# A hybrid decoder trunk on one core: channel sums as one matmul, pooling sums in banks of their own, the last convolution behind the pooling

## The chip, the cores and the metric

The kernel runs on one core of a Trainium2 chip. The metric is device time in microseconds (us), the median of the runs of one kernel on the chip. The engines are PE (TensorE matmuls), PEld (TensorE weight loads), DVE (VectorE), ACT (ScalarE), POOL (GpSimd) and SP (SyncE, which issues most DMAs). Each engine works through its own queue in order and waits on semaphores for the others.

## The reference

One layer for 288 tokens: 256 of a prompt and 8 × 4 sample tokens, which have a history.

```python
h = rmsnorm(x, norm1_g)
proj = h @ w_in + b_in                                  # 2048 -> 3072
a, gate, z = proj[:1024], proj[1024:2048], proj[2048:]  # columns
u = a * sigmoid(gate)
c = silu(layernorm(depthwise_causal_conv(history + u, conv_w (31 taps), conv_b), ln_g, ln_b))
d = multiscale_pool(history + z)      # windows 2, 4, 8, 16 for four groups of 256 channels: window mean - z
p = (d per group @ pool_w[g]) * pool_scale
x = x + concat[c, p] @ w_out                            # 2048 -> 2048
x = x + relu(rmsnorm(x, norm2_g) @ w_ff1) ** 2 @ w_ff2  # 2048 -> 8192 -> 2048
y = rmsnorm(x, norm_f)
```

`rmsnorm` divides by the root of the mean square over the 2048 channels, `layernorm` over the 1024 of the convolution. The outputs are y, the last 30 u and the last 15 z per sequence.

## The kernel before

Channels lie on the 128 partitions, the 288 tokens along the free dimension, so x is 16 tiles (xT) of 128x288. All matmuls take weights of 128x128 as the stationary operand and 288 tokens as the moving one, and fill a PSUM bank `ac` of 128x288. Numbers are split into two parts of a faster format: ScalarE casts a weight block of 128x1024 to `whi` (line 235), VectorE or GpSimd subtracts it from the original to give `wlo` (line 236), and each product is three matmuls, hi × hi, lo × hi, hi × lo (lines 242 to 244). Activations are split the same way (hh and hl, dh and dl, ph and pl, mh and ml, ah and al, fh and fl). There are four buffers each of whi and wlo, four PSUM banks `ac`, two banks `cv` and two banks `ms`.

The order of work on TensorE, in blocks of 256 output columns (a gemm):

- a first stage of 8 steps c, two input tiles each, for convolution channels 0 and 1 (`first_banks`, line 314). x and weights come in together, step by step. 12 warming matmuls of two passes each run ahead of it;
- gemms for conv 2 to 7 (`CONVS`), each giving a and gate of 128 channels, then for pool groups 3, 2, 1, 0 (`POOLS`), 96 matmuls each;
- the pool matmuls of the four groups, 12 each;
- w_out: eight groups of 48 matmuls on the pooling half (bringing in ph and pl), then eight on the convolution half (mh and ml), each added to xT;
- four rounds of ff1 (eight groups) and ff2 (eight groups), 96 matmuls a group.

The norms' factors are applied behind the matmuls. For that, `rsqrt_rows` needs a sum over channels and a root for each of the 288 tokens. It sums with one-column matmuls (`pt`, line 203; three of 96 tokens, on 96 partitions), takes the root on 96x3 elements with a Newton step (lines 211 to 218, tile `st`), writes the result on a diagonal (`dg`, line 220) and spreads it to all partitions with a matmul (`pr`, line 227). It is used four times: for rb (first norm), for the layernorm in w_out (`norm_end`), for r2 (ff1) and for the final norm (rf).

A convolution's gate (`conv_gates`) multiplies both banks by rb, takes the sigmoid `tg` and writes u into `uz`. The 31 taps (`conv_taps`, line 368) then run on VectorE, two channels' chains in turns, with a low priority; their sums end in the tiles `c`, and GpSimd adds these up to `sum_c`. `pmean` (line 440) averages sum_c over channels in w_out's third group. A pool group (`pool_group`) multiplies its bank by rb, writes z to uz, and then puts the windows' sums into the same bank b (line 407), down to dl (line 415).

The program is written in this order, but a scheduler places instructions on each engine's queue by its own estimate of times and by priorities; buffers of a pool are handed out as they come free.

Of the kernel before, what the change touches and what calls it, by code (L numbers as in the profile page):

```python
# [21 lines left out]
TB = T // 3  # L22
# [19 lines left out]
CONVS, POOLS = (2, 3, 4, 5, 6, 7), (3, 2, 1, 0)  # L42
GROUPS = (3, 2, 1, 0)


def weight_blocks():
# [6 lines left out]
    for i in CONVS:  # L53
        yield from w_in(i * P, DC + i * P)
    for g in POOLS:
        yield from w_in(2 * DC + 2 * g * P, 2 * DC + (2 * g + 1) * P)
# [23 lines left out]
def trunk_kernel(ctx: ExitStack, tc: tile.TileContext, io):  # L80
# [58 lines left out]
    squares = uz[:, 0 : KT * T].rearrange("p (k t) -> p k t", t=T)  # L139
# [19 lines left out]
    def load_first(c, cuts=((0, 2),)):  # L159

        raw = raw_tile()
        to = raw[:].rearrange("p (b k) n -> p b k n", b=2)
        src = io["w"][2 * (c // 4) : 2 * (c // 4) + 2].rearrange("b p k n -> p b k n")
        for k0, k1 in cuts:
            nc.sync.dma_start(xT[:, 2 * c + k0 : 2 * c + k1, :], io["xT"][:, 2 * c + k0 : 2 * c + k1, :])
            at = 2 * (c % 4)
            nc.sync.dma_start(to[:, :, k0:k1, :], src[:, :, at + k0 : at + k1, :])
        return raw
# [13 lines left out]
    few = const.tile([P, 1], F32, name="few")  # L182

# [6 lines left out]
    for j in range(12):  # L190
        nc.tensor.matmul(warm[:, 0:P], ones, ones, start=True, stop=True)
    ident = const.tile([TB, TB], F32, name="ident")
    make_identity(nc, ident)
# [5 lines left out]
    def token_sums(parts, pt):  # L199

        for j in range(3):
            for n, t in enumerate(parts):
                nc.tensor.matmul(pt[:TB, j : j + 1], t[:, j * TB : (j + 1) * TB], ones[:, 0:1], start=n == 0, stop=n == len(parts) - 1)  # L203

    def rsqrt_rows(parts, scale, after=None):

        pt = ms("pt", 3)
        token_sums(parts, pt)
        st = const.tile([TB, 4, 3], F32, name=nm("st"))
        s = [st[:, n, :] for n in range(4)]  # L210
        nc.vector.tensor_scalar(s[0], pt[:TB, 0:3], scale, EPS, op0=ALU.mult, op1=ALU.add)
        nc.scalar.activation(s[1], s[0], AF.Sqrt)
        if after is not None:
            load_table(after, s[1][:, 0:1])
        nc.vector.reciprocal(s[2], s[1])
        nc.vector.tensor_tensor(s[3], s[2], s[2], op=ALU.mult)
        nc.vector.scalar_tensor_tensor(out=s[3], in0=s[3], scalar=-0.5, in1=s[0], op0=ALU.mult, op1=ALU.mult)  # L217
        nc.vector.scalar_tensor_tensor(out=s[2], in0=s[3], scalar=1.5, in1=s[2], op0=ALU.add, op1=ALU.mult)
        dg = tmp("dg")
        nc.vector.tensor_tensor(  # L220
            dg[:TB, :].rearrange("p (j t) -> p j t", t=TB),
            ident[:, None, :].to_broadcast([TB, 3, TB]),
            s[2][:, :, None].to_broadcast([TB, 3, TB]),
            op=ALU.mult,
        )
        pr = ms("pr")
        nc.tensor.matmul(pr[:, :T], ones[:TB, :], dg[:TB, :], start=True, stop=True)  # L227
        return pr
# [17 lines left out]
    def gemm(banks, rhs, m_outer=False):  # L246
# [6 lines left out]
        for k, m in order:  # L253
            product(banks[m], rhs[k], get(k, m), k == 0, k == n - 1)
# [12 lines left out]
    def weight_groups():  # L267

        V, G = nc.vector, nc.gpsimd
        for _ in range(len(CONVS) + len(POOLS)):  # L270
            yield halves([split(raw, G) for _ in range(2) for raw in load()])
# [14 lines left out]
    first_banks = bank2() + [bank("cv", cvp, "cv") for _ in range(2)]  # L286
    for c in range(8):
        pair = []
        for k in range(2 * c, 2 * c + 2):
            hh, hl = act("hh"), act("hl")  # L290
            nc.scalar.activation(hh, xT[:, k, :], AF.Copy, scale=v("norm1_g", k))
            nc.vector.scalar_tensor_tensor(out=hl, in0=xT[:, k, :], scalar=v("norm1_g", k), in1=f32(hh), op0=ALU.mult, op1=ALU.subtract)
            pair.append((hh, hl))
        raw = first_raw[c]
        if c == 0:
            hi = wspl.tile([P, 4, 256], F32R, name=nm("whi"), tag="whi")
            lo = wspl.tile([P, 4, 256], F32R, name=nm("wlo"), tag="wlo")
            views = [t[:].rearrange("p (b k) n -> p b k n", b=2) for t in (raw, hi, lo)]
            for k in range(2):
                r, h, l = [t[:, :, k, :] for t in views]  # L300
                nc.scalar.copy(h, r)
                nc.vector.tensor_tensor(l, r, h.bitcast(F32), op=ALU.subtract)
        else:
            hi, lo = split(raw, nc.vector if c < 5 else nc.gpsimd)
# [73 lines left out]
    for i in CONVS:  # L378
# [5 lines left out]
        if i % 2:  # L384
            conv_taps((i - 1, i))
# [209 lines left out]
```

## Time and profile before

| | |
|---|---|
| median of 3 runs | 1130.59 us (1129.89 to 1130.7) |
| profiled execution | 1128.56 us, span 1126.4 us |
| TensorE busy | 1095.7 us, 97% |
| VectorE busy | 643.2 us, 57% |
| ScalarE busy | 473.1 us, 42% |
| GpSimd busy | 173.8 us, 15% |
| mean granted TensorE clock | 0.986 |

The span is the part that the profiler records, from the first to the last instruction; the profiled execution's own time lies 2.2 us around it. Shares are averages over the span. Matmul durations overlap, so TensorE's pace is read from counts over a stretch of time. In rows of groups, the columns are busy time and mean duration in ns of one, and behind the last bar the idle time ahead of them with what ended it. In rows of time, they are the start, the duration, and in brackets the idle time before and its releaser.

### The profile page before, as it was taken

What the parts mean: (1) busy time and instruction counts of PE and PEld (TensorE: products, weight loads), DVE (VectorE), ACT (ScalarE), POOL (GpSimd) and SP (SyncE); (2) the same over time, 40 slices, a digit from 0 to 9 for tenths busy, and PEclk for the clock granted to TensorE, in tenths of its full rate; (3) what the DMA queues carried; (4) which work ended last, traced back from release to release, by engine and by line L of the source; (5) the groups of instructions that cost most, each with busy time, mean ns of one, the idle gap of its engine ahead of it and who ended that gap; (6) DMA issues with size and microseconds to landing.
All of it is one profiled execution on the core that took longest, in us unless ns stands there. A gap on an engine that the chain in (4) does not pass through costs nothing.

```text
span 1126.4 us, 19701 instructions
## 1 busy us (share of the span) xinstructions
PE 1095.7 (97%) x8182; PEld 1090.9 (97%) x8182; DVE 643.2 (57%) x974; ACT 473.1 (42%) x650; POOL 173.8 (15%) x111
## 2 busy tenths in 40 slices
PE   9899968999999999999999999999999999999995
PEld 8899968999999999999999999999999999999995
DVE  7699999477655444444455444454544444554553
ACT  8443434465454433334444333444433334444441
POOL 3899945820000000000000000000000000000000
PEclk9999988999999999999999999999999999999998
DMA  9655726555555555555555555555555555555532
GB/s 322 205 167 171 212 95 156 159 166 165 167 167 165 161 165 168 168 169 166 162 166 164 166 169 168 166 166 162 165 166 169 168 165 163 167 165 166 168 95 84
DMA packets 56665, 187.04 MB, mean 166 GB/s; under 512 B 5888, under 2 KB 11008, under 8 KB 56576
## 3 DMA queue, kind: packets, MB, share of 16 engines
q1 hardware_dynamic: 56432, 185.74, 52.9%
q8 instruction: 64, 1.05, 0.4%
q14 instruction: 25, 0.20, 0.0%
q10 hardware_dynamic: 144, 0.05, 0.0%
HBM read 181.49 MB, written 4.28 MB: 165 GB/s over the span
## 4 chain that ended last, share of the span: by engine, by line
PE 93%; DVE 4%; DMA 1%; issue 1%; ACT 0%; SPq 0%; DVEq 0%
PE ac L242 31%; PE ac L244 31%; PE ac L243 30%; DVE pc L368 1%; DVE ac L407 1%; PE ac L314 1%; PE cv L314 1%; DMA xT<-in_xT 1%; DVE xT L535 0%; DVE s L405 0%; PE pr L227 0%; DVE dg L220 0%; PE pt L203 0%; DVE pl L432 0%; DVE st L217 0%
## 5 line engine op out<-in xcount | busy, mean ns | idle before, releaser
L235 ACT CAST whi<-wr 128x1024 fp32r<-128x1024 f32 x337 | 354.4, 1052 | 594.3 <-PE ac L243 561.0
L236 DVE TENSOR_TENSOR wlo<-wr,whi 128x1024 fp32r<-128x1024 f32 x276 | 338.4, 1226 | 377.6 <-ACT whi L235 377.4
L242 PE MATMUL ac<-ah,whi 128*128 128x288 f32 x1024 | 303.1, 296 | 0.0
L242 PE MATMUL ac<-fh,whi 128*128 128x288 f32 x1024 | 302.6, 296 | 0.0
L244 PE MATMUL ac<-ah,wlo 128*128 128x288 f32 x1024 | 302.0, 295 | 0.0
L244 PE MATMUL ac<-fh,wlo 128*128 128x288 f32 x1024 | 301.7, 295 | 0.0
L243 PE MATMUL ac<-fl,whi 128*128 128x288 f32 x1024 | 300.6, 294 | 0.0
L243 PE MATMUL ac<-al,whi 128*128 128x288 f32 x1024 | 300.0, 293 | 0.0
L243 PEld LDWEIGHTS ac<-fl,whi 128*128 128x128 f32 x1024 | 193.0, 188 | 0.0
L243 PEld LDWEIGHTS ac<-al,whi 128*128 128x128 f32 x1024 | 192.8, 188 | 0.1
L242 PEld LDWEIGHTS ac<-ah,whi 128*128 128x128 f32 x1024 | 192.5, 188 | 0.1
L244 PEld LDWEIGHTS ac<-fh,wlo 128*128 128x128 f32 x1024 | 192.3, 188 | 0.0
L242 PEld LDWEIGHTS ac<-fh,whi 128*128 128x128 f32 x1024 | 192.3, 188 | 0.0
L244 PEld LDWEIGHTS ac<-ah,wlo 128*128 128x128 f32 x1024 | 191.9, 187 | 0.0
L236 POOL TENSOR_TENSOR wlo<-wr,whi 128x1024 fp32r<-128x1024 f32 x61 | 149.9, 2473 | 63.1 <-ACT whi L235 62.8
L242 PE MATMUL ac<-hh,whi 128*128 128x288 f32 x320 | 95.3, 300 | 8.7 <-DVE dl L415 8.7
L368 DVE SCALAR_TENSOR_TENSOR pc<-uz,vec,pc 128x256 f32<-128x256 f32 x232 | 97.7, 485 | 1.5 <-ACT pc L357 1.0
L243 PE MATMUL ac<-hl,whi 128*128 128x288 f32 x320 | 95.1, 299 | 0.0
L244 PE MATMUL ac<-hh,wlo 128*128 128x288 f32 x320 | 92.9, 299 | 0.0
L242 PEld LDWEIGHTS ac<-hh,whi 128*128 128x128 f32 x320 | 61.3, 192 | 9.1 <-DVE dl L415 8.9
L243 PEld LDWEIGHTS ac<-hl,whi 128*128 128x128 f32 x320 | 61.7, 193 | 0.0
L244 PEld LDWEIGHTS ac<-hh,wlo 128*128 128x128 f32 x320 | 60.8, 193 | 0.1
(133 smaller groups left out, 888.6 us busy)
## 6 DMA issues: line engine op xcount, KB each, us to landing
wr<-in_w SPq DMA_DIRECT2D x337, 512.0 KB, 3.8
xT<-in_xT SPq DMA_DIRECT2D x7, 288.0 KB, 8.0
out_u_out<-uz SPq DMA_DIRECT2D x1, 1208.0 KB, 9.6
out_yT<-xT SPq DMA_DIRECT2D x2, 576.0 KB, 2.9
uz<-in_hist_c SPq DMA_DIRECT2D x1, 1088.0 KB, 8.5
out_z_out<-uz SPq DMA_DIRECT2D x1, 668.0 KB, 8.6
uz<-in_hist_p SPq DMA_DIRECT2D x1, 608.0 KB, 9.8
out_yT<-xT SPq DMA_DIRECT2D x2, 288.0 KB, 2.6
```

What stands on the lines that cost most here:

```text
L235: nc.scalar.copy(hi[:, a:b, :], raw[:, a:b, :])
L236: eng.tensor_tensor(lo[:, a:b, :], raw[:, a:b, :], hi[:, a:b, :].bitcast(F32), op=ALU.subtract)
L242: nc.tensor.matmul(b, wh, xh, start=first, stop=False)
L243: nc.tensor.matmul(b, wh, xl, start=False, stop=False)
L244: nc.tensor.matmul(b, wl, xh, start=False, stop=last)
L314: nc.tensor.matmul(first_banks[m][:, :T], lhs(w, k, m), pair[k][x], start=c == 0 and k == 0 and w is hi and x == 0, stop=c == 7 and k == 1 ...
L368: nc.vector.scalar_tensor_tensor(out=dst, in0=u_all[:, i, w : w + SEQ], scalar=cw[i][:, w : w + 1], in1=pc[i], op0=ALU.mult, op1=ALU.add)
L407: nc.vector.tensor_reduce(b[:, 0:SEQ], windows(s[:, at:], (1, SEQ), (step, n)), axis=AX.X, op=ALU.add)
```

## The change

1. x is loaded in seven pieces ahead of most weights of the first stage, its first tile on ScalarE's DMA queue; steps 0 and 1 are split by tile. Eight instead of 12 warming matmuls. All lo parts of the first stage are made on VectorE, and the squares are summed there by running additions. The convolution's history is loaded before the first stage.
2. `rsqrt_rows` works on 128x288 elements: a channel sum is one matmul with a 128x128 matrix of ones, whose result stands on all partitions. ScalarE takes the root from the bank, VectorE does a reciprocal, the Newton step (with the total scaled in place) and a second reciprocal; no diagonal and no second matmul. The sums stand at other places on TensorE: `total` in step 7 of the first stage, `pss` inside the first ff1 group, the final sum `pf` in two parts, the first inside the last gemm.
3. Pooling sums go to banks of their own (`d`, the two banks ms); the bank `ac` is only read until z is written.
4. `SEQUENCE`: conv 2 to 6, then the four pool groups, then conv 7. The taps of conv 6 and of conv 7 are chains of their own.

The diff, cut to its core:

```diff
-CONVS, POOLS = (2, 3, 4, 5, 6, 7), (3, 2, 1, 0)
+SEQUENCE = [("conv", i) for i in range(2, 7)] + [("pool", g) for g in GROUPS] + [("conv", 7)]
...
-    first_raw = [load_first(0, ((0, 1), (1, 2)))]
-    for c in range(1, 6):
-        first_raw.append(load_first(c))
+    load_first(0, 0, 1)
+    load_x(0, 1, nc.scalar)
+    load_x(1, 1)
+    load_first(0, 1, 2)
+    load_x(2, 2)
+    load_first(1, 0, 1)
+    load_first(1, 1, 2)
+    load_x(4, 4)
+    load_first(2)
+    load_x(8, 4)
+    load_first(3)
+    load_x(12, 4)
     nc.sync.dma_start(vec[:, CWO:NV], io["vec"][:, CWO:NV])
-    for c in range(6, 8):
-        first_raw.append(load_first(c))
+    for c in range(4, 8):
+        load_first(c)
+    nc.sync.dma_start(u_all[:, :, UO:UL], io["hist_c"])
...
-    for j in range(12):
+    for j in range(8):
         nc.tensor.matmul(warm[:, 0:P], ones, ones, start=True, stop=True)
...
+    def token_sum(bank, t, first=True, last=True):
+        nc.tensor.matmul(bank[:, :T], ones, t, start=first, stop=last)
+
+    def rsqrt_rows(bank, out, scale, after=None):
+        s1, s2 = tmp("s"), tmp("s")
+        b = bank[:, :T]
+        nc.scalar.activation(s1, b, AF.Sqrt, bias=eps[:, 0:1], scale=scale)
         if after is not None:
-            load_table(after, s[1][:, 0:1])
+            load_table(after, s1[:, 0:1])
+        nc.vector.tensor_scalar(b, b, scale / 2, EPS / 2, op0=ALU.mult, op1=ALU.add)
+        nc.vector.reciprocal(s2, s1)
+        nc.vector.tensor_tensor(b, b, s2, op=ALU.mult)
+        nc.vector.scalar_tensor_tensor(out=s2, in0=s1, scalar=0.5, in1=b, op0=ALU.mult, op1=ALU.add)
+        nc.vector.reciprocal(out, s2)
...
-    nc.scalar.copy(rb, rsqrt_rows(tot, 1.0 / D, AF.Sigmoid)[:, :T])
+    rsqrt_rows(total, rb, 1.0 / D, AF.Sigmoid)
...
-            b = bk[m][:, :T]
-            nc.vector.tensor_tensor(b, b, rb, op=ALU.mult)
+            p = bk[m][:, :T]
+            nc.vector.tensor_tensor(p, p, rb, op=ALU.mult)
...
+            b = ms("d")[:, :T]
...
+    for kind, i in SEQUENCE:
+        (conv_group if kind == "conv" else pool_group)(i)
+        if kind == "conv" and (i % 2 or i == 6):
+            conv_taps((i,) if i >= 6 else (i - 1, i))
...
-        rl = rsqrt_rows([ssc], 1.0 / DC, AF.Silu)
+        rl = ms("rl")
+        token_sum(rl, ssc)
+        rsqrt_rows(rl, rl[:, :T], 1.0 / DC, AF.Silu)
...
-                nc.scalar.copy(r2, rsqrt_rows([ss2], 1.0 / D)[:, :T])
+                rsqrt_rows(pss, r2, 1.0 / D)
...
+                gemm(bk, fx, m_outer=True, hooks={16: lambda: evict(0), 28: lambda: token_sum(pf, ssf, last=False)})
...
-    rf = rsqrt_rows([ssf, qf], 1.0 / D)
+    rf = row("rf")
+    rsqrt_rows(pf, rf, 1.0 / D)
```

The scheduler's order at three places. First, TensorE around the first norm's sum. Before, pr stands inside conv 2's gemm (banks 610 and 611):

```order
L242 MATMUL ac_610<-hh_251,whi_481 128x288
L243 MATMUL ac_610<-hl_252,whi_481 128x288
L244 MATMUL ac_610<-hh_251,wlo_482 128x288
L242 MATMUL ac_611<-hh_251,whi_481 128x288
L243 MATMUL ac_611<-hl_252,whi_481 128x288
L227 MATMUL pr_515<-dg_513,ones 128x288
L244 MATMUL ac_611<-hh_251,wlo_482 128x288
L242 MATMUL ac_610<-hh_284,whi_481 128x288
```

After, TensorE's only work for the norm is `total`, inside step 7 of the first stage (first_banks are ac_160, ac_161, cv_162, cv_163):

```order
L321 MATMUL ac_160<-hl_359,whi_356 128x288
L321 MATMUL ac_161<-hl_359,whi_356 128x288
L321 MATMUL cv_162<-hl_359,whi_356 128x288
L321 MATMUL cv_163<-hl_359,whi_356 128x288
L210 MATMUL total_164<-tot_456,ones 128x288
L321 MATMUL ac_160<-hl_363,whi_356 128x288
L321 MATMUL ac_161<-hl_363,whi_356 128x288
```

A matmul behind the root has become one ahead of it, and it stands in the first stage.

Second, VectorE in the pooling. Before, ac_1608 and ac_1609 are the banks of one pool group, ac_1758 and ac_1759 those of the next, and pc the taps' sums:

```order
L409 TENSOR_TENSOR ac_1609<-ac_1609,rise 128x15
L410 SCALAR_TENSOR_TENSOR ac_1608<-ac_1608,uz 128x256
L399 TENSOR_TENSOR ac_1758<-ac_1758,rb_497 128x288
L368 SCALAR_TENSOR_TENSOR pc_1203<-uz,vec,pc_1203 128x256
L399 TENSOR_TENSOR ac_1759<-ac_1759,rb_497 128x288
L368 SCALAR_TENSOR_TENSOR pc_1200<-uz,vec,pc_1200 128x256
L410 SCALAR_TENSOR_TENSOR ac_1609<-ac_1609,uz 128x256
L412 SCALAR_TENSOR_TENSOR ac_1608<-ac_1608,uz 128x32
```

After, the same stretch of a pool group's work, with its sums in d_1555 and d_1570, and the next group's banks ac_1582 and ac_1583:

```order
L404 TENSOR_TENSOR d_1570<-d_1570,rise 128x15
L393 TENSOR_TENSOR ac_1582<-ac_1582,rb_499 128x288
L374 SCALAR_TENSOR_TENSOR pc_1189<-uz,vec,pc_1189 128x256
L393 TENSOR_TENSOR ac_1583<-ac_1583,rb_499 128x288
L405 SCALAR_TENSOR_TENSOR d_1555<-d_1555,uz 128x256
L374 SCALAR_TENSOR_TENSOR pc_1192<-uz,vec,pc_1192 128x256
L405 SCALAR_TENSOR_TENSOR d_1570<-d_1570,uz 128x256
L374 SCALAR_TENSOR_TENSOR pc_1189<-uz,vec,pc_1189 128x256
L407 SCALAR_TENSOR_TENSOR d_1555<-d_1555,uz 128x32
```

The work is the same and stands in the same turns; what moved is the bank that it holds.

Third, ScalarE ahead of the second half of w_out, whose operands are mh and ml (cc is the silu of n, the normed convolution). Before, casts of weights stand between the pairs of cc and mh, and whi_2966, of the convolution half's second group, ahead of the last mh:

```order
L460 ACTIVATE cc_2691<-n_2687,vec 128x288
L461 CAST mh_2673<-cc_2675 128x288
L235 CAST whi_2901<-wr_2897 128x1024
L460 ACTIVATE cc_2699<-n_2695,vec 128x288
L461 CAST mh_2681<-cc_2683 128x288
L460 ACTIVATE cc_2707<-n_2703,vec 128x288
L461 CAST mh_2689<-cc_2691 128x288
L235 CAST whi_2905<-wr_2899 128x1024
L460 ACTIVATE cc_2715<-n_2711,vec 128x288
L461 CAST mh_2697<-cc_2699 128x288
L461 CAST mh_2705<-cc_2707 128x288
L235 CAST whi_2966<-wr_2962 128x1024
```

After, whi_2893 and whi_2897 are the convolution half's first group, whi_2958 and whi_2962 its second, and the row above them loads ScalarE's table behind the root of rl:

```order
L196 ACTIVATE few<-s_2638 128x1
L230 CAST whi_2893<-wr_2889 128x1024
L230 CAST whi_2897<-wr_2891 128x1024
L230 CAST whi_2958<-wr_2954 128x1024
L230 CAST whi_2962<-wr_2956 128x1024
L470 ACTIVATE cc_2651<-n_2647,vec 128x288
L470 ACTIVATE cc_2659<-n_2655,vec 128x288
L471 CAST mh_2649<-cc_2651 128x288
L471 CAST mh_2657<-cc_2659 128x288
```

All four casts now come ahead of the first cc. On VectorE, two of the blocks' lo parts and the second reciprocal, which gives rl, stand as follows to the first n and ml:

```order
L222 SCALAR_TENSOR_TENSOR s_2639<-s_2638,rl_2636 128x288
L231 TENSOR_TENSOR wlo_2898<-wr_2891,whi_2897 128x1024
L223 RECIPROCAL rl_2636<-s_2639 128x288
L231 TENSOR_TENSOR wlo_2959<-wr_2954,whi_2958 128x1024
L467 TENSOR_TENSOR n_2647<-c_523,rl_2636 128x288
L479 TENSOR_TENSOR xT<-xT,ac_2839 128x288
L479 TENSOR_TENSOR xT<-xT,ac_2840 128x288
L467 TENSOR_TENSOR n_2655<-c_526,rl_2636 128x288
L231 TENSOR_TENSOR wlo_2963<-wr_2956,whi_2962 128x1024
L467 TENSOR_TENSOR n_2663<-c_855,rl_2636 128x288
L472 TENSOR_TENSOR ml_2650<-cc_2651,mh_2649 128x288
```

Here ac_2839 and ac_2840 are the banks of the pooling half's last group; the xT additions for them now stand between the first n and the second.

More of the change, by code (lines that the diff above doesn't have):

```diff
@@ L197, in trunk_kernel @@
             nc.gpsimd.memset(rise[:, g, t : t + 1], w / (t + 1))
[L199 to L212, printed above, removed]
[L213 to L228 removed]
+    nc.gpsimd.memset(u_all[:, :, 0:CH], 0.0)
+    def token_sum(bank, t, first=True, last=True):
[4 more added lines that the diff above has]
+        nc.scalar.activation(s1, b, AF.Sqrt, bias=eps[:, 0:1], scale=scale)
+        if after is not None:
+            load_table(after, s1[:, 0:1])
[4 more added lines that the diff above has]
+        nc.vector.reciprocal(out, s2)
     def split(raw, eng, cuts=((0, 4),)):
@@ L294, in trunk_kernel @@
[L294 to L304, printed above, removed]
@@ L516, in trunk_kernel, with evict @@
             bk = bank2()
-            gemm(bk, fx, m_outer=last and g == 7)
-            for m in range(2):
+            def evict(m):
                 k = 2 * g + m
```

128 lines of the change are left out of this document (74 added, 54 removed).

## The prediction

> **What bounds the kernel now.** I read the page's head first, then the chain and the waits, and then asked for a table by stretches cut at the places where TensorE stands still.
>
> ```profile
> span 1126.4 us, 19701 instructions
> PE 1095.7 (97%) x8182; PEld 1090.9 (97%) x8182; DVE 643.2 (57%) x974; ACT 473.1 (42%) x650; POOL 173.8 (15%) x111
> ```
>
> TensorE is busy for 97% of the span, so the kernel is bound by its 8112 main matmuls (the rest are the warming ones and the sums), which the change leaves alone. Time can come only from stretches in which TensorE is idle or has half its clock. The table gives, for each stretch, busy time by engine with instructions in brackets, the granted clock, the DMA share and GB/s.
>
> ```profile
> 6.12:34.82 28.70, 27.53 (x207) 26.70 (x206) 20.99 (x22) 22.41 (x35) 14.78 (x7) 1.00 0.94 338
> 34.82:46.97 12.15, 7.91 (x48) 7.42 (x48) 9.58 (x10) 3.65 (x6) 8.65 (x4) 0.87 0.84 285
> 46.97:143.46 96.49, 96.42 (x726) 96.19 (x725) 88.02 (x201) 42.16 (x58) 90.76 (x42) 1.00 0.55 172
> 143.46:156.20 12.74, 4.13 (x17) 4.13 (x18) 12.74 (x31) 3.04 (x7) 2.56 (x2) 0.60 0.29 85
> 156.20:179.40 23.20, 23.20 (x176) 23.20 (x175) 21.64 (x58) 10.91 (x17) 17.61 (x9) 1.00 0.42 132
> 179.40:193.75 14.35, 10.70 (x52) 8.78 (x51) 14.35 (x42) 6.58 (x14) 5.37 (x3) 0.77 0.79 166
> 245.90:1111.87 865.97, 865.97 (x6540) 865.86 (x6539) 434.69 (x529) 351.42 (x462) 0.00 (x0) 1.00 0.52 161
> 1111.87:1126.40 14.53, 2.58 (x16) 1.58 (x14) 6.99 (x13) 1.18 (x3) 0.00 (x0) 0.62 0.41 162
> 400.00:700.00 300.00, 300.00 (x2266) 300.00 (x2266) 142.14 (x160) 111.59 (x131) 0.00 (x0) 1.00 0.54 166
> ```
>
> The last row gives the price of a matmul at full clock, 300.00/2266 = 0.1324 us. From 245.90 to 1111.87, 77% of the span, nothing can be won. Four stretches lose time: 34.82–46.97, 143.46–156.20, 179.40–193.75 and the tail. TensorE's waits (total, times, longest) name their causes:
>
> ```profile
> PE ac L242 <- DVE dl L415: 8.7, 1, 8.7
> PE pr L227 <- DVE dg L220: 6.0, 2, 4.2
> PE ac L242 <- DVE pl L432: 2.5, 4, 0.9
> PE pt L203 <- ACT q L527: 0.9, 1, 0.9
> ```
>
> **The change part by part.** All terms are against the profiled execution (span 1126.4, time 1128.56), which is 2.03 us below the median of the runs, 1130.59.
>
> *1, reciprocal roots of the first norm.* Before, TensorE stood 4.2 us at pr, with conv 2's matmuls queued behind it. Now the channel sum is one matmul inside the first stage's last step, and nothing behind it on TensorE waits for the roots until conv 3 wants a bank, 96 matmuls or 12.7 us later. Of the stretch's 48 matmul records two are pr; the other 46 stay: 12.15 − 46 × 0.1324 gives **−6.06**.
>
> *2, banks of the pooling sums.* The 8.7 us wait is for dl, the last reader of a bank that the pooling arithmetic kept; the 60% clock is its aftermath. Now the bank is free when z is written. The stretch holds 17 matmuls: 12.74 − 17 × 0.1324 = **−10.49**. Its cover is VectorE's pace. From 46.97 to 193.75 VectorE worked 88.02 + 12.74 + 21.64 + 14.35 = 136.75 us. With conv 7 last, that conv's taps and gates and the pooling outputs' splits fall behind the last pool:
>
> ```profile
> L368 DVE SCALAR_TENSOR_TENSOR pc<-uz,vec,pc 128x256 f32<-128x256 f32 x232 | 97.7, 485 | 1.5 <-ACT pc L357 1.0 <-issue 0.5
> L432 DVE SCALAR_TENSOR_TENSOR pl<-ac,vec,ph 128x288 fp32r<-128x288 f32 x8 | 4.2, 520 | 0.0
> ```
>
> These are 30 taps, whose starts lie some 0.4 us apart where pairs interleave (12 to 14 us), 4.2 us of splits and about 3 us of gates and reduction, some 20 us. So about 116 us of VectorE work must fit between 36 and 162, where the pool matmuls begin: 126 us, 10 us to spare. If that cover is gone, the pool matmuls wait for dl as before (a rival).
>
> *3, around the pool matmuls.* This stretch lost 14.35 − 52 × 0.1324 = 7.47 us. It now follows conv 7, and has waits of its own. Pool group 2's banks are those of conv 7, freed by its gate, and on ScalarE the gate's sigmoid is queued behind both ph of group 3, which need that group's 12 matmuls:
>
> ```profile
> L431 ACT ACTIVATE ph<-ac,vec 128x288 fp32r<-128x288 f32 x8 | 4.0, 501 | 8.0 <-PE ac L244 8.0
> L343 ACT ACTIVATE tg<-ac,vec 128x288 f32<-128x288 f32 x7 | 3.5, 496 | 0.1
> L186 ACT ACT_TABLE_LOAD x4 | 5.1, 1283 | 1.2 <-PEq L577 1.2
> ```
>
> Two ph and a sigmoid are 1.5 us after those matmuls, with a step 1.6 idle; the gated product on VectorE, for the second bank, another 0.4; a table load (1.28) in front of the next ph some 0.3 to 0.5. I take 2.5 us idle and 1.0 for the clock. −7.47 + 3.5 = **−4.0**.
>
> The clock's price is read here, in two stretches inside it:
>
> ```profile
> 183.50:186.92 3.42, 1.88 (x12) 1.41 (x11) 3.42 (x13) 1.95 (x3) 1.53 (x1) 1.00 1.04 178
> 186.92:190.33 3.41, 2.46 (x8) 1.80 (x8) 3.41 (x13) 0.81 (x3) 0.84 (x1) 0.52 1.13 178
> ```
>
> After a stretch in which TensorE was 55% busy, the next 3.41 us had about half the clock. A full such stretch costs 3.41/2 = 1.7 us. The Trainium skill, "TensorE: Matmul & The Clock Gate", section "What's actually happening", lets the clock fall after at least one idle window of about 3.4 us; by it the waits of this term and of 5, which share windows with work, cost no clock, and the sum would be 2.7 lower. This trace differs: the stretch ahead of the fall held 1.88 us of work.
>
> *4, small edits.* Fewer warming matmuls, x ahead of the weights, the first loads: the first stage runs on DMA at 0.94 share and 338 GB/s, the same bytes arrive, and 27.53 of 28.70 us are busy; between a loss of 2.5 (rival E) and a gain of 1.2, the idle part, I take −0.3, since the columns of pt leave. In w_out and the first ff1 group pt goes, and one sum like pmean comes in the place of pr, which was as large:
>
> ```profile
> 212.79 0.65 PE L440 MATMUL pmean<-sum_c,avg 128*128 128x288 f32 x2
> 1113.05 0.33 PE L203 MATMUL pt<-ones,q 128*96 128x1 f32 x2 [0.93 <-ACT q L527]
> ```
>
> Three pairs of pt, overlapping, are about 0.4 each time; the last gemm takes in the first half of the final sum, +0.4. The history load is only earlier. **−0.7**.
>
> *5, a new wait in w_out.* Between the halves of w_out, ScalarE now has four weight casts ahead of the first cc, the last two (whi_2958, whi_2962) for the conv half's second group, and VectorE has four weight splits, four xT adds and both reciprocals of 128x288 between the root and the first ml. Before, only one cast of those two was ahead of the last mh, and the halves met without a wait. The weights have four buffers: one of the two casts can start in the middle of the pool half's last group, the other only when that half's last matmul is over (T below), as before:
>
> ```profile
> 242.95 1.05 ACT L235 CAST whi<-wr 128x1024 fp32r<-128x1024 f32 x1 [0.79 <-issue]
> 243.90 0.43 ACT L461 CAST mh<-cc 128x288 fp32r<-128x288 f32 x1
> 246.08 1.05 ACT L235 CAST whi<-wr 128x1024 fp32r<-128x1024 f32 x1 [1.75 <-PE ac L243]
> 247.17 1.23 DVE L236 TENSOR_TENSOR wlo<-wr,whi 128x1024 fp32r<-128x1024 f32 x1 [0.50 <-ACT whi L235]
> L457 DVE TENSOR_TENSOR n<-c,pr 128x288 f32<-128x288 f32 x8 | 3.4, 446 | 1.7 <-PE pr L227 1.6
> L460 ACT ACTIVATE cc<-n,vec 128x288 f32<-128x288 f32 x8 | 4.8, 624 | 1.8 <-DVE n L457 1.7
> L461 ACT CAST mh<-cc 128x288 fp32r<-128x288 f32 x8 | 3.3, 421 | 0.0
> ```
>
> The pool half ended at 245.90, the cast began 0.18 later. The price also needs R, a reciprocal of 128x288, which this trace lacks. Its nearest rows:
>
> ```profile
> L215 DVE RECIPROCAL st<-st 96x3 f32<-96x3 f32 x3 | 0.5, 174 | 1.0 <-ACT st L212 1.0
> L211 DVE TENSOR_SCALAR st<-pt 96x3 f32<-96x3 f32 x3 | 0.5, 156 | 3.0 <-PE pt L203 3.0
> ```
>
> Bounds: 0.45 (an ordinary pass, as n) and 16.7 (174 ns for 3 elements, all of it per element). The reciprocal is 18 ns over the pass beside it for 3 elements, 6.0 ns each, and a pass grows by (446 − 156)/285 = 1.0 ns: 156 + 288 × 7.0 = **2.2 us**, which I take as the difference between like rows. The Trainium skill, "VectorE: DVE Perf Modes", section "First, the fixed hardware budget", has the reciprocal as an iterative divide with a repeat count of 8; at one step per 1.0 ns that would be an estimated 2.5 us, and the sum 1.2 higher. No run here shows it yet.
>
> The chain, from T: the sum rl stands 80 matmuls ahead, its root is there at −9.6. VectorE: total scaled −9.2, R −7.0, a split −5.8, product and two xT adds −4.4, Newton step −3.9, a split −2.65, R −0.45, a split 0.8, first n 1.25, two xT adds 2.15, second n 2.6, a split 3.85, third n 4.3, first ml 4.75. ScalarE: cast to 1.23, cc 1.9, cc 3.25, mh 3.65. TensorE waits 3.65 for mh, does four matmuls and waits 0.55 for ml: **+4.2**; with R at 0.45 it is 3.2, and above 2.2 both reciprocals count, 2 us per us. One stretch at half clock, between 0 and 3.4: **+1.7**.
>
> *6, the tail.* From the last matmul (1111.87) to the first multiply:
>
> ```profile
> 1112.55 0.44 ACT L527 ACTIVATE q<-xT 128x288 f32<-128x288 f32 x1 [5.36 <-DVE xT L521]
> 1115.82 1.33 PE L227 MATMUL pr<-dg,ones 96*128 96x288 f32 x2 [1.76 <-DVE dg L220]
> 1117.19 5.28 DVE L535 TENSOR_TENSOR xT<-xT,pr 128x288 f32<-128x288 f32 x6 [1.42 <-PE pr L227]
> ```
>
> After: sum from 1113.05, 0.65 and a step as pmean, 1113.74; root 0.5 (as tg); four VectorE passes of 0.45 with steps, 1115.8; and two R. 1115.8 + 4.4 = 1120.2 against 1117.19: **+3.0**. What follows stays.
>
> Sum: −6.06 − 10.49 − 4.0 − 0.7 + 4.2 + 1.7 + 3.0 = −12.35. Span 1114.0, this execution 1116.2, median 1130.59 − 12.35 = **1118.2 us**. With R from 0.45 to 3 and the clock terms from 0 to twice, 1112 to 1124.
>
> **The rivals.** *A, the wait at T is not there:* mixc is ready early, as when before's mh ended by 244. Against: the order of the two engines. −5.9: 1112.3. *B, VectorE becomes the bound:* 10 us to spare on 126 is little, and GpSimd's subtractions run beside it; half of term 2 returns, 1123.4. *C, slower:* the reciprocals at width 288. Four of them lie on ends (two before T, two in the tail), so each us above 2.2 costs 4, and the gain is gone at R = 2.2 + 12.35/4 = 5.3 us, 18 ns per element; at 8 us it is 1141. For it speaks the upper bound, against it the 18 ns that three elements cost over a plain pass. *D, the clock doesn't fall in the waits of 2.5 and 4 us,* since no stretch of 3.41 us is idle all through: −2.7, 1115.5. Against it stands the row at 183.50. It is the rule of the Trainium skill's page cited in 3. *E, the first stage starves:* 16 in place of 24 warming passes leave a gap before the first weights and a half clock, and steps 0 to 4 wait for weights behind x: +2.5, 1120.7.
>
> **How the numbers follow.** Forecast 0.53, A 0.10, B 0.13, C 0.05, D 0.12, E 0.07. The range leaves out C and the outer ends of A and B: 1111 to 1126. Two thousandths, 2.3 us, is about what a measurement tells from no change: all cases but C are faster by more; C lies within it at R from 4.7 to 5.9. Faster 0.93, same 0.02, slower 0.05.
>
> **What would show it.** Term 1: no wait of TensorE on a sum or root near 35–47. Term 2: no wait on dl, TensorE full from 34 to about 161. Term 3: two short waits on tg and the gated product. Term 5: about 4 us on mh and ml near 223, half clock behind. Term 6: a RECIPROCAL of 128x288 at 2.2 us and 8.3 us from the last matmul to the first multiply. Wrong if reciprocals take 5 us, if TensorE waits on dl, or if ScalarE's mh are done before T.

## The result, and the profile after

The changed kernel takes **1109.82 us** (median of 4 runs, 1109.09 to 1111.32), against 1130.64 for the kernel before in the same series; the ratio is 0.9818 (95% interval 0.9801 to 0.9835), 20.8 us or 1.8% faster. The forecast was 1118.2 with a range of 1111 to 1126, so it missed on the low side. The profiled execution took 1111.32 us, 1.5 above its own median.

The head of the page after, and its waits of TensorE (total, times, longest):

```profile
span 1109.5 us, 19621 instructions
PE 1086.3 (98%) x8140; PEld 1083.9 (98%) x8140; DVE 648.2 (58%) x982; ACT 472.8 (43%) x648; POOL 162.8 (15%) x106
...
PE ac L237 <- ACT mh L471: 2.4, 1, 2.4
PE ac L321 <- DVE hh L305: 1.3, 1, 1.3
PE ac L237 <- DVE pl L440: 1.1, 2, 0.9
...
PE pf L210 <- ACT q L540: 1.0, 1, 1.0
PE ac L237 <- ACT tg L349: 1.0, 1, 1.0
```

The waits for dl (8.7) and for dg (6.0) are gone, and a wait for mh has come. The table by stretches, now cut at the start of main matmuls 192, 288 (conv 2 between them), 672, 1056 (the four pool groups), 1152, 1200 (the pool matmuls), 1584, 1600 (T and the first 16 matmuls of the convolution half) and the last one, 8112:

```profile
33.52:46.25 12.73, 12.73 (x98) 12.73 (x97) 9.83 (x25) 5.68 (x9) 12.73 (x6) 1.00 0.61 197
97.46:148.56 51.10, 51.10 (x386) 51.10 (x385) 47.39 (x102) 23.46 (x37) 42.46 (x20) 1.00 0.55 173
161.25:169.42 8.17, 6.90 (x50) 6.44 (x49) 7.99 (x19) 7.21 (x13) 7.84 (x5) 1.00 0.76 236
222.22:228.41 6.19, 3.81 (x19) 3.59 (x17) 5.94 (x15) 5.95 (x12) 0.00 (x0) 0.72 0.50 170
1092.07:1109.46 17.39, 1.04 (x5) 0.35 (x3) 10.95 (x12) 1.48 (x3) 0.00 (x0) 0.59 0.34 136
400.00:700.00 300.00, 300.00 (x2267) 300.00 (x2266) 142.78 (x160) 110.90 (x130) 0.00 (x0) 1.00 0.53 166
```

From such rows a loss is worked out for each stretch: its length less the number of main matmuls between its two cuts at 0.1324 us. Conv 2 is 12.73 − 96 × 0.1324 = 0.02 now, the pool matmuls 8.17 − 48 × 0.1324 = 1.82. For the two kernels (each profiled twice, below) and the main experiments, in us:

| kernel | first stage, 1–192 | conv 2, 192–288 | 672–1056 | pool matmuls, 1152–1200 | 1200–1584 | T, 1584–1600 | 2352–8112 | last main matmul to the end |
|---|---|---|---|---|---|---|---|---|
| before | 2.43 | 7.33 | 11.15 | 7.64 | 1.63 | 0.00 | 0.55 | 14.71 |
| before, again | 11.49 | 1.37 | 10.79 | 7.63 | 3.03 | 0.00 | 0.55 | 14.14 |
| after | 2.12 | 0.02 | 0.26 | 1.82 | 1.95 | 4.08 | 1.03 | 17.39 |
| after, again | 2.09 | 0.02 | 0.26 | 1.82 | 2.14 | 2.74 | 1.03 | 17.39 |
| banks | 1.42 | 0.02 | 12.99 | 1.23 | 0.94 | −0.02 | 1.03 | 17.38 |
| order | 1.93 | 0.02 | 0.36 | 9.38 | 1.66 | −0.02 | −4.48 | 17.38 |
| roots | 2.37 | 0.50 | 0.26 | 1.82 | 2.70 | 0.00 | 0.55 | 14.85 |
| order_roots | 2.21 | 0.50 | 0.36 | 9.37 | 2.67 | −0.01 | 0.55 | 14.28 |
| start | 1.80 | 0.01 | 0.29 | 1.83 | 1.48 | 9.48 | −4.28 | 17.37 |
| newton | 1.56 | 0.02 | 0.26 | 1.83 | 2.14 | −0.01 | −4.48 | 15.87 |

The spans fell by 17.0 (1126.44 to 1109.46): −7.3 in conv 2, −10.9 at the pooling banks, −5.8 at the pool matmuls, +4.1 at T, +2.7 at the end, +0.3 in all the rest, some of which the table leaves out.

The place T in the timeline (start, duration; idle time and its releaser in brackets), first ScalarE, then VectorE, then TensorE:

```profile
222.41 1.05 ACT L230 CAST whi<-wr 128x1024 fp32r<-128x1024 f32 x1 [2.05 <-PE ac L238]
223.37 1.14 ACT L470 ACTIVATE cc<-n,vec 128x288 f32<-128x288 f32 x2
224.41 0.75 ACT L471 CAST mh<-cc 128x288 fp32r<-128x288 f32 x2
...
221.85 0.44 DVE L467 TENSOR_TENSOR n<-c,rl 128x288 f32<-128x288 f32 x1
222.21 0.81 DVE L479 TENSOR_TENSOR xT<-xT,ac 128x288 f32<-128x288 f32 x2
...
224.88 1.33 PE L237 MATMUL ac<-mh,whi 128*128 128x288 f32 x4 [2.38 <-ACT mh L471]
```

This is the chain that the prediction described: the last cast starts when the pool half's matmuls end, both cc and mh follow it, TensorE waits for mh. But VectorE's first n ends 0.07 us behind T and not 1.25, so ScalarE goes from cast to cc without a pause. And the reciprocals, by group (mean ns of one behind the bar):

```profile
L220 DVE RECIPROCAL s<-s 128x288 f32<-128x288 f32 x4 | 7.8, 1943 | 0.0
L223 DVE RECIPROCAL rl<-s 128x288 f32<-128x288 f32 x1 | 2.0, 1953 | 0.0
```

The tail, with the final sum, the second reciprocal and the first multiply:

```profile
1093.38 0.75 PE L210 MATMUL pf<-q,ones 128*128 128x288 f32 x2 [1.02 <-ACT q L540]
1098.05 1.95 DVE L223 RECIPROCAL rf<-s 128x288 f32<-128x288 f32 x1
1100.03 1.13 DVE L558 TENSOR_TENSOR xT<-xT,rf 128x288 f32<-128x288 f32 x2
```

### The profile page after: what moved, and what is told of

It reads as the page before. It is cut to its first block, busy times and chain, and to the rows that moved or that the text cites. A ratio compares the mean times of both kernels' runs of the same rounds, so it can differ in the third digit from the quotient of the medians.

```text
span 1109.5 us, 19621 instructions
## 1 busy us (share of the span) xinstructions
PE 1086.3 (98%) x8140; PEld 1083.9 (98%) x8140; DVE 648.2 (58%) x982; ACT 472.8 (43%) x648; POOL 162.8 (15%) x106
## 3 DMA queue, kind: packets, MB, share of 16 engines
q8 instruction: 63, 1.03, 0.4%
HBM read 181.49 MB, written 4.28 MB: 167 GB/s over the span
## 4 chain that ended last, share of the span: by engine, by line
PE 97%; DVE 2%; ACT 0%; DMA 0%; issue 0%; DVEq 0%
PE ac L237 32%; PE ac L239 31%; PE ac L238 31%; PE ac L321 1%; PE cv L321 1%; DVE xT L558 0%; DMA wr<-in_w 0%; DVE pc L374 0%; DVE pl L440 0%; DVE rf L223 0%; DVE s L220 0%; PE pf L210 0%; DVE c L369 0%; ACT cc L470 0%; ACT whi L230 0%
## 5 line engine op out<-in xcount | busy, mean ns | idle before, releaser
L230 ACT CAST whi<-wr 128x1024 fp32r<-128x1024 f32 x330 | 346.9, 1052 | 597.3 <-PE ac L238 566.4
L231 DVE TENSOR_TENSOR wlo<-wr,whi 128x1024 fp32r<-128x1024 f32 x272 | 333.3, 1225 | 373.0 <-ACT whi L230 372.6
L231 POOL TENSOR_TENSOR wlo<-wr,whi 128x1024 fp32r<-128x1024 f32 x58 | 138.8, 2406 | 29.0 <-ACT whi L230 28.6
L239 PE MATMUL ac<-hh,wlo 128*128 128x288 f32 x320 | 89.1, 295 | 0.0
```

Of the source, the lines that this page charges most:

```text
L230: nc.scalar.copy(hi[:, a:b, :], raw[:, a:b, :])
L231: eng.tensor_tensor(lo[:, a:b, :], raw[:, a:b, :], hi[:, a:b, :].bitcast(F32), op=ALU.subtract)
L239: nc.tensor.matmul(b, wl, xh, start=False, stop=last)
```

## The experiments

The theory: three waits went by the parts named in terms 1 to 3 (roots, banks, order), and the wide reciprocals cost at T and in the tail. The rivals: a part did not do it, but the earlier x or less work on VectorE; or the miss lies in the executions compared and not in the parts. Every experiment but before_again starts from the kernel after and changes what its diff shows.

**banks**: the pooling sums in the bank of the product again.

```diff
-            b = ms("d")[:, :T]
+            b = p
```

> The changed kernel with the pooling sums back in the gemm's own banks; all else as changed. Theory (the bank's last reader sets the wait): in the changed kernel's trace pool group 3's lo parts are made at 128.3 to 129.6 us, and group 1's gemm, which would need those two banks, starts at about 123.2: TensorE waits on dl about 5.6 us, and one stretch at half clock adds 1 to 1.7; the later groups then find their banks free. 6 to 8 us slower than the changed kernel. Rival (putting conv 7 last already gives VectorE the time, the banks add nothing): within 1 us of the changed kernel, no wait on dl.

Measured: 1117.6 us, ratio to before 0.9886 (0.9870 to 0.9903), 7.8 slower than after. Its wait of TensorE, and the stretch behind it:

```profile
PE ac L237 <- DVE dl L410: 10.5, 1, 10.5
127.00:137.60 10.60, 4.58 (x19) 4.58 (x20) 10.60 (x28) 1.60 (x4) 0.00 (x0) 0.52 0.15 47
```

The wait for dl is back and larger than the 5.6 us expected, with a half clock of some 10 us behind it: 12.99 in the table against 0.26. Some of it comes back at T, where the engines now have caught up (−4.1). Term 2's cause is shown.

**order**: conv 7 ahead of the pools, the taps of 6 and 7 paired.

```diff
-SEQUENCE = [("conv", i) for i in range(2, 7)] + [("pool", g) for g in GROUPS] + [("conv", 7)]
+SEQUENCE = [("conv", i) for i in range(2, 8)] + [("pool", g) for g in GROUPS]
...
-        if kind == "conv" and (i % 2 or i == 6):
-            conv_taps((i,) if i >= 6 else (i - 1, i))
+        if kind == "conv" and i % 2:
+            conv_taps((i - 1, i))
```

> The changed kernel with conv 7 back ahead of the four pool groups and its taps paired with those of conv 6; pooling sums stay in their own banks. Theory (VectorE's pace sets the pool matmuls, and conv 7's place is what makes room): no wait on banks inside the pool gemms, but the pool matmuls, which TensorE reaches at about 161, wait on the last group's dl, since some 145 us of VectorE work from 36 on must come first (181): a wait of 10 to 15 us moved there, with half clock behind it; 10 to 16 us slower than the changed kernel. Rival (the banks alone remove the wait): within 2 us of the changed kernel.

Measured: 1108.5 us, ratio 0.9802 (0.9787 to 0.9817): 1.3 *faster* than after. Its wait, and its pace in the long gemms:

```profile
PE ac L237 <- ACT dh L409: 5.2, 2, 4.9
400.00:700.00 300.00, 300.00 (x2283) 300.00 (x2282) 143.19 (x161) 111.79 (x131) 0.00 (x0) 1.00 0.53 167
```

The local effect is there: the pool matmuls lose 9.38 in place of 1.82, T loses nothing. But 2283 matmuls in the 300 us, not 2267, save 5.5 us in the long gemms, in which this kernel and after do the same work. The medians alone would have given the wrong sign. At equal pace the part is worth 7.56 less the 4.1 or 2.7 of T (two profiles of after), 3.5 to 4.8 us beside the new roots: a wait came at the place where one was expected, on dh in place of dl, but the expected 10 to 16 us were far too much.

**roots**: the old way to the roots (pt, st, dg, pr) at all four places, everything else as after.

```diff
-    def rsqrt_rows(bank, out, scale, after=None):
+    def rsqrt_rows(parts, scale, after=None):
...
-                if c == 7 and w is lo:
-                    token_sum(total, rows[0])
...
-    rsqrt_rows(pf, rf, 1.0 / D)
+    rf = rsqrt_rows([ssf, qf], 1.0 / D)
```

> The changed kernel with the old route to the reciprocal roots (column sums, 96x3 elements, diagonal, second matmul) in all four places; banks, order and loads as changed. Theory (the new route wins at the first norm alone and loses at the other ends): +6.1 for the wait on pr in the first gemm behind the first stage, +0.8 for the columns in w_out and ff1, -3.7 for the wait on mh between the halves of w_out, which goes since no reciprocal of 128x288 stands ahead of n, -2.8 in the tail: +0.4, the same as the changed kernel within 1 us, and no wait on mh. Rival (the new route is a gain at every place): 5 to 9 us slower, the wait on mh stays.

Measured: 1105.84 us, ratio 0.9778 (0.9764 to 0.9793), 4.0 faster than after, at the ordinary pace of 2267, where +0.4 was expected: the 6.1 us for a wait on pr did not come. Conv 2 loses only 0.50 with the old way: the 6 us that it cost before are not in the way itself. VectorE's rows for the first norm in before, one of GpSimd's of before, then the same in roots:

```profile
35.43 0.17 DVE L215 RECIPROCAL st<-st 96x3 f32<-96x3 f32 x1 [0.27 <-ACT st L212]
35.63 0.89 DVE L216 TENSOR_TENSOR st<-st 96x3 f32<-96x3 f32 x1
36.56 2.31 DVE L217 SCALAR_TENSOR_TENSOR st<-st 96x3 f32<-96x3 f32 x1
38.90 2.28 DVE L218 SCALAR_TENSOR_TENSOR st<-st 96x3 f32<-96x3 f32 x1
41.29 2.49 DVE L220 TENSOR_TENSOR dg<-ident,st 96x288 f32<-96x288 f32 x1
31.76 11.70 POOL L236 TENSOR_TENSOR wlo<-wr,whi 128x1024 fp32r<-128x1024 f32 x5
...
27.96 0.16 DVE L230 TENSOR_TENSOR st<-st 96x3 f32<-96x3 f32 x1
28.34 0.16 DVE L232 SCALAR_TENSOR_TENSOR st<-st 96x3 f32<-96x3 f32 x1
28.61 0.46 DVE L234 TENSOR_TENSOR dg<-ident,st 96x288 f32<-96x288 f32 x1
29.22 9.49 POOL L250 TENSOR_TENSOR wlo<-wr,whi 128x1024 fp32r<-128x1024 f32 x4 [6.84 <-ACT whi L249]
```

In before, the last four of GpSimd's five subtractions end at 36.51, 38.86, 41.17 and 43.47, and each of VectorE's passes with two operands in SBUF ends just behind such an end, at 36.52, 38.87, 41.18 and 43.78. In roots the sum is there earlier (the first pt at 25.40 against 34.03); the passes are done at 29.07, before GpSimd begins, and take 0.16 us, the one for dg 0.46. The Trainium skill, "SBUF — State Buffer", section "🔬 SBUF: two separate sides", has the rule: a VectorE operation with two SBUF inputs and a GpSimd operation that reads SBUF lock each other out for a whole instruction. This trace agrees, and the reciprocal, with one input, took 0.17 beside GpSimd.

**start**: x and weights of the first stage in turns as before the change, 12 warming matmuls, the new roots kept.

```diff
+    load_x(0, 1)
     load_first(0, 0, 1)
-    load_x(0, 1, nc.scalar)
...
-    load_x(4, 4)
-    load_first(2)
-    load_x(8, 4)
-    load_first(3)
-    load_x(12, 4)
+    for c in range(2, 6):
+        load_x(2 * c, 2)
+        load_first(c)
...
-    for c in range(4, 8):
+    for c in range(6, 8):
+        load_x(2 * c, 2)
         load_first(c)
...
-    for j in range(8):
+    for j in range(12):
```

> The changed kernel with x and the weights of the first stage loaded in turns as before, on one queue, and 12 warming matmuls; all else as changed. Theory (the first stage gained 1.2 us from the loads, and lost as much to the half clock that 8 warming matmuls leave from 6.1 to 9.5 us in the profiled execution): first stage 1 us later by the loads, 1.2 to 1.7 us earlier by the clock, so within 1 us of the changed kernel, with the first matmuls at full clock. Rival (loads matter, warming does not): 1 to 2 us slower.

Measured: 1110.74 us, ratio 0.9819 (0.9804 to 0.9834). The first norm's sum, and the wait:

```profile
31.36 0.65 PE L209 MATMUL total<-tot,ones 128*128 128x288 f32 x2
PE ac L236 <- ACT mh L470: 7.5, 1, 7.5
```

The sum is 6.1 us later than in after (25.25), so the early x brings it forward by that much, and conv 2 still loses nothing: the new way's wide passes kept 0.45 and 0.47 us beside GpSimd, which fits that rule, as one of their two operands lies in a PSUM bank. T loses more instead, 9.48 against 4.08: the reciprocal that gives rb starts 5.1 us later (36.13 against 31.05), the first n 4.9 (226.77 against 221.85). That the one delay is the other is read from these rows and not tested. The median lies within 1 us of after, as expected, by luck: this program too ran its long gemms at the faster pace (2282 in the 300 us, −5.3 us). With before, roots and after this is a square: the loss in conv 2 is 7.33 with the old way and a late sum (1.37 in before's second profile, below), 0.50 old and early, 0.01 new and late, 0.02 new and early. Either half is enough for term 1.

**newton**: the second reciprocal replaced by a Newton step on the first one.

```diff
-        nc.vector.tensor_scalar(b, b, scale / 2, EPS / 2, op0=ALU.mult, op1=ALU.add)
+        nc.vector.tensor_scalar(b, b, scale, EPS, op0=ALU.mult, op1=ALU.add)
         nc.vector.reciprocal(s2, s1)
-        nc.vector.tensor_tensor(b, b, s2, op=ALU.mult)
-        nc.vector.scalar_tensor_tensor(out=s2, in0=s1, scalar=0.5, in1=b, op0=ALU.mult, op1=ALU.add)
-        nc.vector.reciprocal(out, s2)
+        nc.vector.tensor_tensor(s1, s2, s2, op=ALU.mult)
+        nc.vector.scalar_tensor_tensor(out=s1, in0=s1, scalar=-0.5, in1=b, op0=ALU.mult, op1=ALU.mult)
+        nc.vector.scalar_tensor_tensor(out=out, in0=s1, scalar=1.5, in1=s2, op0=ALU.add, op1=ALU.mult)
```

> The changed kernel with the second reciprocal of 128x288 replaced by a Newton step in three ordinary passes, in all four places. Theory (the reciprocals are on the two ends that the new route lost): a reciprocal is 1.95 us and a pass 0.46, so the tail is 1.5 us shorter; ahead of the second half of w_out the root comes 1.5 us earlier and the scheduler now puts a mh ahead of the last weight cast, so that the wait of 2.4 us on mh falls to 1 us or less and the clock stays up: -2.5 there. 3.5 to 4.5 us faster than the changed kernel. Rival (the wait on mh is set by the weight cast alone): -1.5, the wait stays.

Measured: 1100.21 us, ratio 0.9727 (0.9714 to 0.9741), the best version. ScalarE at T:

```profile
220.16 1.14 ACT L470 ACTIVATE cc<-n,vec 128x288 f32<-128x288 f32 x2
221.21 0.75 ACT L471 CAST mh<-cc 128x288 fp32r<-128x288 f32 x2
222.31 1.05 ACT L230 CAST whi<-wr 128x1024 fp32r<-128x1024 f32 x1 [0.35 <-PE ac L238]
```

Two mh now stand ahead of the last cast, and T loses nothing (−4.1, or −2.7 against after's second profile); the tail is 1.5 shorter. The rest of the 9.6 us is pace: 2284 matmuls in the 300 us, −5.5, which nothing in the edit explains.

**order_roots**: both edits at once, for the price of the order at equal pace.

> Two parts of the change undone together: conv 7 ahead of the pools again, and the old route to the roots everywhere; pooling sums in own banks and the early sums of squares stay. Theory (with conv 7 first, VectorE's pace alone sets the last dl, and the four reciprocals and passes of the new route at the first norm are 4 us of it): against conv 7 first alone, the waits of 6.1 us on dh and dl fall to some 2, their half clock from 3 to 1.5, and the tail is 2.8 shorter: 1100 to 1102 us. Rival (VectorE is not the bound there; the parts add up without touching each other): conv 7 first was 1.3 us better than the changed kernel and the old roots 4.0, so 1104.5.

Measured: 1113.22 us, ratio 0.9845 (0.9832 to 0.9859), pace 2267 as roots:

```profile
PE ac L256 <- ACT dh L425: 5.3, 2, 5.0
```

Against roots, also without a wait at T, conv 7 ahead of the pools costs 7.4 us, 7.55 of it at the pool matmuls. The wait for dh is as long as in order, so the time that the wide reciprocals take on VectorE has no part in it: what was expected of that fell. In order VectorE stands idle for 1.09 us ahead of its first gate at 34.34, waiting for TensorE's bank, so those reciprocals were over before they could delay anything. What sets the wait for dh stays open.

**before_again**, **after_again**: the two kernels unchanged, a second profile of each.

> The kernel before, unchanged, profiled once more. Open: the profiled execution that the prediction was summed against lies 2 us below the median of the others. Theory (executions differ by where the half-clock stretches of 3.41 us fall): matmul counts per stretch and waits as in the first profile, a span of 1128 to 1129.5, and the 2 us stand in one more stretch at half clock or in the first stage. Rival (the first profile was of another pace of TensorE throughout): 400 to 700 us holds another count than 2266 matmuls.

> The changed kernel, unchanged, profiled once more. Theory: a span near 1107.5, first stage at full clock from 5 to 6 us on (1.5 us shorter than in the first profile, where half clock lasted to 9.7), the wait on mh of 2.4 us with one half-clock stretch behind it, and 2267 matmuls from 400 to 700. Rival (TensorE's pace of 0.1314 us, seen in three of the experiments, comes with the execution and not with the built program): 2283 matmuls there, and about 1103.

Measured: 1131.11 and 1110.09 us. In before's second profile TensorE waits inside the first stage for lo parts that VectorE makes, and the wait for pr in conv 2 is gone (the 1.8 us left of it are in the tail). TensorE's waits, then GpSimd's and VectorE's rows, and last GpSimd's first subtraction in the first profile:

```profile
PE ac L314 <- DVE wlo L236: 2.8, 2, 2.5
PE ac L314 <- DVE hl L292: 1.9, 2, 1.7
19.80 7.74 POOL L236 TENSOR_TENSOR wlo<-wr,whi 128x1024 fp32r<-128x1024 f32 x3 [17.72 <-ACT whi L235]
20.12 5.21 DVE L292 SCALAR_TENSOR_TENSOR hl<-xT,vec,hh 128x288 fp32r<-128x288 f32 x2
25.25 3.37 DVE L236 TENSOR_TENSOR wlo<-wr,whi 128x1024 fp32r<-128x1024 f32 x1
20.04 6.43 POOL L236 TENSOR_TENSOR wlo<-wr,whi 128x1024 fp32r<-128x1024 f32 x1 [17.95 <-ACT whi L235]
```

It is the same collision at another place. In the second profile GpSimd goes first and VectorE's three passes, each with two operands in SBUF, take 2.67, 2.62 and 3.37 us; in the first they take 0.55, 0.55 and 1.25, and GpSimd's subtraction of 2.4 us takes 6.43. Behind it, in the second profile, the passes of the first norm meet only the end of GpSimd's run (at 44.82): 1.11 us for the first, then 0.16. So the first stage and conv 2 lose 11.49 + 1.37 = 12.9 there and 9.8 in the profile that the prediction started from; since the first matmul starts 1.0 us earlier in the second, conv 2 ends 2.1 us later.

In after the two profiles agree, but for T: the first time the clock fell behind the wait, the second time not. The two stretches of 3.41 us with the wait, cut at the changes of the clock in the trace and at multiples of 3.41 us from them, in after, then in after_again:

```profile
221.28:224.70 3.42, 1.22 (x10) 1.00 (x8) 3.32 (x7) 2.29 (x4) 0.00 (x0) 1.00 0.59 211
224.70:228.11 3.41, 3.23 (x13) 3.23 (x14) 3.34 (x10) 3.37 (x8) 0.00 (x0) 0.50 0.49 163
220.69:224.10 3.41, 1.95 (x15) 1.73 (x14) 3.31 (x7) 1.55 (x3) 0.00 (x0) 1.00 0.60 209
224.10:227.51 3.41, 2.49 (x18) 2.43 (x19) 3.41 (x9) 3.37 (x9) 0.00 (x0) 1.00 0.59 211
```

The wait is 2.38 us in both. In after it leaves one stretch 36% busy, and the next one has half the clock; in after_again it lies over two, 57% and 73%, and the clock stays. So the 1.3 us between them is where the wait happens to lie. The busy share alone doesn't decide it: in order the clock fell behind a stretch that was 63% busy (165.46 to 168.87), in before_again it stayed behind one of 61% (185.03 to 188.45).

**warm12** (after) and **roots_warm12** (roots) with 12 warming matmuls:

```diff
-    for j in range(8):
+    for j in range(12):
```

> The changed kernel with 12 instead of 8 warming matmuls, nothing else. Theory (warming only keeps the clock up until the first main matmul): 0 to 1 us faster than the changed kernel by the first stage; the wait on mh grows by what the first stage gains, so that the end moves less: the same within 0.5 us. Rival (where an instruction stands in TensorE's stream decides its pace in the long gemms; this moves all by 16): 2283 matmuls from 400 to 700 us instead of 2267, 5 to 6 us faster.

> The changed kernel with the old route to the roots and 12 instead of 8 warming matmuls. Theory (with 8, the last warming matmul ends at 4.8 us and the first main ones run at half clock to 9.5 us in some executions): the first stage ends 1 us earlier: 0.5 to 1.2 us faster than with 8. Rival (what loads last ends the first stage, so the clock at its start is made up): the same within 0.3 us.

Measured: 1111.14 (ratio 0.9825, 0.9812 to 0.9838) and 1104.97 us (0.9769, 0.9756 to 0.9783), +1.3 and −0.9 against their bases: opposite signs, so no effect of the warming can be told, and both keep the ordinary pace.

**newton_warm12** and **newton_again** (newton unchanged), five executions each, on the pace.

> One reciprocal with a Newton step, and 12 warming matmuls. Theory (its 1100.2 us with 8 hold 5.5 us of a faster pace in the long gemms that no part of the edit explains): if the pace stays, 1099.5 to 1100.5, the best version; if it is the ordinary one, 1105 to 1106, still 4 us faster than the changed kernel by the wait on mh and the tail. Rival (all of the 9.6 us come from the roots): 1099.5 to 1100.5 with the ordinary count of 2267 matmuls from 400 to 700 us.

> The same program as newton, once more, five executions. What is asked is the pace of the long gemms. If the pace belongs to the built program, all executions lie at 1099.7 to 1100.4 and the stretch 400 to 700 holds 2283 or 2284 matmuls. If it goes with the execution, as the two at 1106 of newton_warm12 suggest, one or two of the five lie near 1106, and a profile of such a one would hold some 2267. If both paces occur, the gain of newton over after at equal pace is 5.5 less than the medians say, about 4 us: the wait at T (2.7 to 4.1) and 1.5 in the tail.

Measured: medians 1100.27 and 1099.92 us (ratios 0.9754, 0.9729 to 0.9779, and 0.9751, 0.9726 to 0.9777). The single times are 1099.72, 1099.77, 1100.27, 1105.78, 1106.45 and 1099.76, 1099.79, 1099.92, 1105.81, 1106.17. The same program has two times, 6 us apart, so the program alone doesn't fix the pace. The profiles, of executions at 1100, show 2283 matmuls in the 300 us; no execution at 1106 was profiled, so that these had the ordinary pace is inferred from the 5.5 us that it is worth. The five executions of after all lie at 1109.09 to 1111.32; that it has the faster pace too is not shown. At equal pace newton gains about 4 us on after (1106 against 1110). What sets the pace stays open.

## Why the prediction missed

It named the parts and the signs right, and gave too small a gain. From 1130.59 to 1109.82 is −20.8, forecast −12.35; of the 8.4 between, 4.6 lie in the terms, 0.3 in what the span does not record, and 3.5 in the step from one execution to the median.

*The base, the step that failed.* "All terms are against the profiled execution … median 1130.59 − 12.35" takes for granted that this execution loses what the others lose. It was a lucky one: 2.03 us below its median and below every other execution of before on record (lowest 1129.89), while after's lay 1.5 above its own. The second pair of profiles lies within 0.5 us of the medians, and its spans hold the whole gain: 1129.03 − 1108.27 = 20.8. There TensorE comes to the end of conv 2 9.9 us earlier (at 46.20 in place of 56.06), in the first pair 7.7; terms 1 and 4 had 6.06 and 0.3 for it. Term 4 took the first stage's possible gain to be the idle 1.2 us of the profile at hand; in the second profile that stage lost 11.49, 9 us more than in the first, behind VectorE's passes that waited on GpSimd. After the change VectorE makes all lo parts of that stage, and GpSimd's first subtraction comes at 29.05 or later (20.04 and 19.80 before). In the twelve profiles of kernels with that part of the change the first stage lost 1.4 to 2.4, and 1.8 in start, where x comes in turns again. No run gives GpSimd those subtractions back, so that this part of the change and not the loads removes the loss is read from the traces.

*Term 1*, −6.06 forecast, −7.3 measured (−1.3 in the second pair, where the loss stood in the first stage): "12.15 − 46 × 0.1324" counted 46 of the stretch's records as main matmuls, where 43 are (0.4 us), and left out 0.8 us of the pt matmuls ahead of the cut at 34.82. Its cause was half right. The one matmul and its place do remove the wait (start), but so does the early sum with the old way (roots), and what made the old way dear was VectorE waiting on GpSimd, which the prediction read past: 2.31 us for a pass of 96x3.

*Term 2*, −10.49 forecast, −10.9 measured. VectorE kept pace, rival B didn't come. *Term 3*, −4.0 forecast, −5.8 measured up to the cut at 1200 and −4.8 with the 1.0 that a wait on pl of 0.9 costs just behind it: 2.1 us idle in place of 2.5, but only the first wait as argued (1.0 on tg; the other 1.1 on pl, not on the gated product), and no clock lost in place of 1.0, as rival D had it. The Trainium skill's "TensorE: Matmul & The Clock Gate", section "What's actually happening", asks for an idle window; here the trace fits it, since no window was idle all through. Behind T it doesn't: after's clock fell after the 36% busy stretch shown above. Neither the rule nor the prediction's "55%" is enough.

*Term 4*, −0.7 forecast, +0.3 measured over all the rest, −0.7 without that wait on pl. The parts are not all those forecast: the first stage has the −0.3; pt in w_out and in the first ff1 group is worth 0.5 each (forecast 0.4); the column 2352–8112 grew by 0.5 (forecast +0.4 for half of the final sum); and conv 3 to 6 (288–672) grew by 0.4, which no step had.

*Term 5*, +5.9 forecast, +4.1 and +2.7 measured. The mechanism and the place were right, the wait was mis-sized, 2.38 in place of 3.65 + 0.55: passes of 0.45 start 0.37 apart when they follow each other, a reciprocal took 1.95, and ml was in time. The clock's share, 1.7 forecast and 1.3 measured, came in one profile of after and not in the other.

*Term 6*, +3.0 forecast, +2.7 measured (+3.2 in the second pair), with R 1.95 against 2.2. From 3 elements to 288 that is (1943 − 174)/285 = 6.2 ns per element, forecast 7.0. The estimate of 2.5 us from the repeat count of 8 in the Trainium skill's "VectorE: DVE Perf Modes", section "First, the fixed hardware budget", was further off. Rival C was far away. The low end given for R of 0.45 and no clock terms, 1112, comes out as 1111.0 from its own terms (−1.0 at T, −3.5 in the tail, −2.7).

So the new roots, counted as the main gain of the first stage, are a net loss of 4.0 us in the finished kernel: beside an early x they save 0.5 and cost 2.5 in the tail and 2.7 to 4.1 at T; 0.7 to 0.8 us comes back in smaller places.

## What to carry to other kernels

When small VectorE passes take ten times what their like take elsewhere, see what GpSimd does at that moment before redesigning them; moving them ahead of it may be all that is needed. Price an edit by the stretch in which it acts, in two profiles of the kernel before: one execution can be lucky, here by 2 us, and a median holds other things, here a pace worth 5.5 us that made a worse order look 1.3 us faster. When several parts of a change remove the same wait, undo each alone, since the costs of the others remain.

## What the runs showed of the hardware

TensorE has two paces at a granted clock of 1.00: 300/2267 = 0.1323 us and 300/2283 = 0.1314 us for the same matmuls of 128x288, and one program shows times 6 us apart, execution by execution. A VectorE pass with two SBUF operands takes up to 2.31 us in place of 0.16 beside GpSimd's subtractions, one with a single SBUF operand its usual time; which of the two engines is held up differs between executions of one kernel (VectorE's hl 2.67 in place of 0.55 us, or GpSimd's subtraction 6.43 in place of 2.4). A reciprocal of 128x288 takes 1.95 us, an ordinary pass 0.45. The clock fell after stretches of 3.41 us that were 36%, 53% (before, 183.66 to 187.07) and 63% busy, and not after ones of 57%, 61% and 73%.
